# Seven block products in place of eight for half of a down-projection, put between the pieces of the next up-projection

## The chip, the cores and the metric

The kernel runs on one core of a Trainium2 chip. The metric is the device time of one launch in microseconds (us). Matmuls run on TensorE (PE; its weight loads are shown as PEld), elementwise work on VectorE (DVE) and ScalarE (ACT), and all transfers are issued from SyncE's queue (SP).

## The reference

One layer of a hybrid encoder, for a sequence of 256 tokens and a width of 2,048, all in float32. An attention block comes first (eight heads of forgetting attention, eight of stick-breaking attention), then the block that the change is about, a feed-forward block with a short convolution:

```python
def conv_ffn(h, w_up_l, conv_w_l, conv_b_l, w_down_l):
    u = h @ w_up_l                       # (256, 2048) @ (2048, 2 * 5632)
    u = lax.conv_general_dilated(...) + conv_b_l   # causal, depthwise, width 3
    gate, val = jnp.split(u, 2, axis=-1)
    return (jax.nn.silu(gate) * val) @ w_down_l    # (256, 5632) @ (5632, 2048)

x = x + hybrid_mixer(rms_norm(x, attn_norm), ...)
x = x + conv_ffn(rms_norm(x, ffn_norm), w_up, conv_w, conv_b, w_down)
```

## The kernel before

A float32 matmul is made of three matmuls of a rounded type: each operand is split into a high part (`hi`, the value rounded) and a low part (`lo`, what is left), and the products hi x hi, hi x lo and lo x hi are summed in PSUM.

`weights` (L202) brings in every weight: 1 MB (128 partitions of 2,048 values) goes by DMA into one of three `w_raw` buffers, ScalarE casts it into one of two `w_hi` buffers (L210), and VectorE subtracts to make one of two `w_lo` buffers (L211). Its three instructions are written at a raised priority (`AHEAD`), so that the scheduler puts them ahead of other work. The scheduler of the framework sets the order on each engine when the kernel is built, from priorities, from data and from buffers coming free; on the chip each engine runs its list in order.

Two shapes of matmul use these weights. `feature_major` (L242) makes the up-projection: two feature tiles of 128 for all 256 tokens, in two steps of 32 matmuls (16 with a moving operand of 512 columns, L250, 16 of 256, L255), each with one load of weights. `token_major` (L220) makes 512 output columns for two token tiles: each load of weights serves four row tiles, so a chunk is 4 x 2 x 3 = 24 matmuls of 512 columns (L235 to L237). After each step or chunk both call `step()`, which advances generators that hold other work, here the last of the attention.

The feed-forward block takes its 44 feature tiles in three parts of 16, 16 and 12. In each part, pairs of feature tiles come first: `up_pair` for the gate and for the value, `convolved` (L582: the sum of two PSUM halves, the norm's factor `R`, the three taps), SiLU, product, and the split into `g2`, whose tiles wait for the down-projection. Then the part's down-projection runs, four groups of 512 columns, each added to the residual rows `x2` (L630). After the last part each group is stored. The up accumulators rotate over three buffers of two PSUM banks.

The memory is handed out in pools. `const`, `wpool` (the weight buffers), `big` (`x2`, the transposed input `hT`) and `small` live through the kernel; `at` and `tmp` belong to the attention and are closed at its end. The pool `ff` of the feed-forward block is opened after that, on their ground; its first instructions are the MEMSETs of `up` (L579). The attention ends with the out-projection (`token_major` with `oT`, of which the last four tiles lie in `hT`), the update of the rows (L556), the squares of the new rows (L167, into `junk` in `tmp`), and the transposes into `hT` (L152). `crow`, the convolution's parameters, is loaded early (L118, L119) and transposed after the first pair.

Of the kernel before, what the change touches and what calls it, by code (L numbers as in the profile page):

```python
# [11 lines left out]
ALU = mybir.AluOpType  # L12
# [27 lines left out]
FFN_PARTS = [(0, 16), (16, 32), (32, 44)]  # L40
# [3 lines left out]
def hybrid_layer(  # L44
# [28 lines left out]
    wpool = ctx.enter_context(tc.tile_pool(name="wpool", bufs=3))  # L73
# [5 lines left out]
    def f32(t):  # L79
        return t.bitcast(F32)  # L80
# [5 lines left out]
    crow = const.tile([NC2, 4, P], F32, name="crow")  # L86
# [94 lines left out]
    def in_every_partition(dg, n):  # L181
        R = const.tile([P, S], F32, name=f"R{n}")
# [19 lines left out]
    def weights(src, a, b):  # L202
        raw = wpool.tile([P, 2048], F32, name="w_raw", tag="w_raw")
        hi = wpool.tile([P, 2048], F32R, name="w_hi", tag="w_hi", bufs=2)
        lo = wpool.tile([P, 2048], F32R, name="w_lo", tag="w_lo", bufs=2)
        n = a * b
        r3 = raw[:, :n].rearrange("p (a b) -> p a b", a=a)
        with tc.high_priority(offset=AHEAD):
            nc.sync.dma_start(r3, src)
            act.copy(hi[:, :n], raw[:, :n])  # L210
            dve.tensor_tensor(lo[:, :n], raw[:, :n], f32(hi[:, :n]), op=ALU.subtract)  # L211
# [57 lines left out]
    with ExitStack() as actx:  # L269
        at = actx.enter_context(tc.tile_pool(name="at", bufs=1))  # L270
# [201 lines left out]
        R1 = in_every_partition(dg1, 1)  # L472
        R1q = const.tile([P, S], F32, name="R1q")
# [92 lines left out]

    def convolution_parameters():
# [6 lines left out]
    ff = ctx.enter_context(tc.tile_pool(name="ff", bufs=2))  # L574
    psf = ctx.enter_context(tc.tile_pool(name="psf", bufs=1, space=bass.MemoryType.PSUM))
    nu = 4
    up = [ff.tile([P, 2, 2 + S], F32, name=f"up{i}") for i in range(nu)]
    for u in up:
        dve.memset(u[:, :, 0:2], 0.0)  # L579
    n_up = 0  # L580

    def convolved(ps, f0):  # L582

        nonlocal n_up
        u = up[n_up % nu]
# [3 lines left out]
        a = ff.tile([P, 2, S], F32, name="cv", tag="cv", bufs=4)  # L589
# [13 lines left out]
    def up_pair(f0):  # L603

        nonlocal R, n_pair
        pool, tag = (psf, "pu") if n_pair % 3 == 2 else (psa, "acc")
        n_pair += 1
        acc = feature_major(wu, f0 * P, pool, tag)
        if R is None:
            R = in_every_partition(dg2, 2)  # L610
            convolution_parameters()
        return convolved(acc, f0)

    gT = {}
    n_pair = 0
    for n_part, (f_lo, f_hi) in enumerate(FFN_PARTS):
        for f in range(f_lo, f_hi, 2):
            gate = up_pair(f)
            val = up_pair(NFT + f)
            act.activation(gate, gate, AF.Silu)  # L620
            dve.tensor_tensor(gate, gate, val, op=ALU.mult)
            g2 = ff.tile([P, 2, 2, S], F32R, name="g2", tag="g2", bufs=12)
            act.copy(g2[:, 0], gate)  # L623
            dve.tensor_tensor(g2[:, 1], gate, f32(g2[:, 0]), op=ALU.subtract)
            for j in range(2):
                gT[f + j] = g2[:, :, j, :]
        for c in range(4):
            acc = token_major(lambda k: gT[f_lo + k], wd, f_lo, f_hi - f_lo, 512 * c, 512)
            xs = x2[:, :, c * 512 : (c + 1) * 512]
            dve.tensor_tensor(xs, acc, xs, op=ALU.add)  # L630
            if n_part == len(FFN_PARTS) - 1:
                for t in range(NT):
                    nc.sync.dma_start(of[t * P : (t + 1) * P, c * 512 : (c + 1) * 512], xs[:, t, :])
# [57 lines left out]
```

## Time and profile before

| | |
|---|---|
| median of 3 runs | 1152.66 us (1152.63 to 1153.39) |
| the profiled execution | 1153.37 us |
| its span, first to last instruction | 1151.6 us |
| the out-projection ends, the first up step begins | 412.9 us from the start of the span |
| the first part's down-projection begins | 593.3 us |
| moved by DMA | 211.39 MB, mean 184 GB/s |

In the rows of the profile a line stands as "L250", then the engine, the operation, output<-inputs, the count and the busy time. A timeline row begins with the start and the duration in us. A row of busy times by stretch has, after the stretch and its length, the busy time of PE, PEld, DVE, ACT and POOL, each with the count of its instructions, then the granted TensorE clock, the DMA share and GB/s. A wait has the waiting instruction, what it waited for, the total in us, how often, and the longest.

### The profile page before, as it was taken

To read this page: it belongs to the slowest core of one execution; us is meant where nothing else is said; L and a number is where in the kernel's file an instruction comes from. 1 tells how busy PE (TensorE), PEld (TensorE's weight loads), DVE (VectorE), ACT (ScalarE), POOL (GpSimd) and SP (SyncE) were. 2 spreads that over 40 slices of the span, in tenths; PEclk is the share of its full clock that TensorE was granted. 3 is DMA by queue.
4 is the path that set the end of the run, shared out by engine and by line. 5 is a ranking of instruction groups with operands and counts; after the bars stand their busy time and mean duration, and the time that the engine had idled before them with its cause. 6 is when DMAs were issued, how large, how long until landed. Compare 5 with 4: busy or idle time off the path is not lost.

```text
span 1151.6 us, 14371 instructions
## 1 busy us (share of the span) xinstructions
PE 1137.1 (99%) x6002; PEld 976.7 (85%) x6002; DVE 716.4 (62%) x798; ACT 551.9 (48%) x620; POOL 0.2 (0%) x4
## 2 busy tenths in 40 slices
PE   7999999999999999999999999999999999999998
PEld 5998888888888888888888888888888888888886
DVE  4646756646565667677774546767775455767753
ACT  4644454455564555555554334555554334555531
POOL 0000000000000000000000000000000000000000
PEclk9999999999999999999999999999999999999999
DMA  6766555564445545555556655555556655555562
GB/s 227 213 210 204 170 173 161 168 182 148 147 149 170 185 154 193 195 194 185 183 183 198 203 183 186 194 196 192 184 183 188 204 193 183 187 195 193 189 221 74
DMA packets 162540, 211.39 MB, mean 184 GB/s; under 512 B 3737, under 2 KB 117547, under 8 KB 162475
## 3 DMA queue, kind: packets, MB, share of 16 engines
q1 hardware_dynamic: 162474, 210.47, 56.7%
q8 instruction: 47, 0.77, 0.3%
q14 instruction: 19, 0.15, 0.0%
HBM read 208.36 MB, written 2.10 MB: 183 GB/s over the span
## 4 chain that ended last, share of the span: by engine, by line
PE 96%; DVE 1%; ACT 1%; DMA 1%; issue 1%; SPq 0%; ACTq 0%; DVEq 0%
PE pu L250 34%; PE pu L255 17%; PE acc L236 14%; PE acc L237 14%; PE acc L235 14%; ACT w_hi L210 1%; DVE w_lo L211 1%; PE ps_x L152 1%; DMA w_raw<-in_w_in_dram 0%; DMA masks<-in_cst_dram 0%; PE ps_z L492 0%; PE ps_h L284 0%; PE ps_s L425 0%; PE ps_o L452 0%; PE ps_o L518 0%
## 5 line engine op out<-in xcount | busy, mean ns | idle before, releaser
L211 DVE TENSOR_TENSOR w_lo<-w_raw,w_hi 128x2048 fp32r<-128x2048 f32 (+2 forms) x204 | 450.8, 2210 | 360.2 <-ACT w_hi L210 360.2
L210 ACT CAST w_hi<-w_raw 128x2048 fp32r<-128x2048 f32 (+2 forms) x204 | 375.9, 1843 | 512.4 <-issue 260.5
L250 PE MATMUL pu<-hT,w_hi 128*128 128x512 f32 x1664 | 523.5, 396 | 0.0
L255 PEld LDWEIGHTS pu<-hT,w_lo 128*128 128x128 f32 x1664 | 312.4, 188 | 73.9 <-DVE w_lo L211 0.4
L255 PE MATMUL pu<-hT,w_lo 128*128 128x256 f32 x1664 | 327.6, 278 | 0.0
L250 PEld LDWEIGHTS pu<-hT,w_hi 128*128 128x128 f32 x1664 | 253.8, 189 | 0.3
L236 PE MATMUL acc<-w_lo,g 128*128 128x512 f32 x352 | 137.1, 389 | 0.8 <-DVE w_lo L211 0.8
L235 PE MATMUL acc<-w_hi,g 128*128 128x512 f32 x352 | 137.1, 389 | 0.0
L237 PE MATMUL acc<-w_hi,g 128*128 128x512 f32 x352 | 136.9, 389 | 0.0
L235 PE MATMUL acc<-w_hi,hT 128*128 128x512 f32 (+1 forms) x320 | 120.2, 376 | 0.0
L236 PE MATMUL acc<-w_lo,hT 128*128 128x512 f32 (+1 forms) x320 | 119.2, 373 | 0.5 <-DVE w_lo L211 0.3
L237 PE MATMUL acc<-w_hi,hT 128*128 128x512 f32 (+1 forms) x320 | 119.0, 372 | 0.0
L236 PEld LDWEIGHTS acc<-w_lo,g 128*128 128x128 f32 x352 | 66.1, 188 | 14.8 <-DVE w_lo L211 1.3
L235 PEld LDWEIGHTS acc<-w_hi,g 128*128 128x128 f32 x352 | 66.1, 188 | 13.8 <-ACT g L623 0.3
L237 PEld LDWEIGHTS acc<-w_hi,g 128*128 128x128 f32 x352 | 66.1, 188 | 13.8
L597 DVE SCALAR_TENSOR_TENSOR cv<-up,ccol,cv 128x256 f32<-128x256 f32 x176 | 74.2, 480 | 2.2 <-ACT cv L592 2.0
L236 PEld LDWEIGHTS acc<-w_lo,hT 128*128 128x128 f32 x320 | 60.5, 189 | 9.6 <-DVE w_lo L211 1.5
L237 PEld LDWEIGHTS acc<-w_hi,hT 128*128 128x128 f32 x320 | 60.6, 189 | 8.8
L235 PEld LDWEIGHTS acc<-w_hi,hT 128*128 128x128 f32 x320 | 60.6, 189 | 8.1
L592 ACT ACTIVATE cv<-up,ccol 128x256 f32<-128x256 f32 x88 | 48.2, 591 | 8.0 <-DVE up L588 8.0
L235 PE MATMUL acc<-w_hi,oT 128*128 128x512 f32 x96 | 38.1, 397 | 0.0
L237 PE MATMUL acc<-w_hi,oT 128*128 128x512 f32 x96 | 37.5, 390 | 0.0
(146 smaller groups left out, 602.4 us busy)
## 6 DMA issues: line engine op xcount, KB each, us to landing
w_raw<-in_w_up_dram SPq DMA_DIRECT2D x88, 1024.0 KB, 5.1
w_raw<-in_w_down_dram SPq DMA_DIRECT2D x44, 1024.0 KB, 5.1
w_raw<-in_w_in_dram SPq DMA_DIRECT2D x36, 1024.0 KB, 5.3
w_raw<-in_w_out_dram SPq DMA_DIRECT2D x16, 1024.0 KB, 5.1
w_raw<-in_w_in_dram SPq DMA_DIRECT2D x12, 688.0 KB, 4.3
w_raw<-in_w_in_dram SPq DMA_DIRECT2D x8, 512.0 KB, 5.3
out_dram<-x SPq DMA_DIRECT2D x8, 256.0 KB, 3.6
x<-in_x_dram SPq DMA_DIRECT2D x3, 512.0 KB, 6.2
```

The lines of the kernel that those rows point to most:

```text
L152: nc.tensor.transpose(ps[:, j, t * P : (t + 1) * P], xt[t][:, (k + j) * P : (k + j + 1) * P], ident)
L210: act.copy(hi[:, :n], raw[:, :n])
L211: dve.tensor_tensor(lo[:, :n], raw[:, :n], f32(hi[:, :n]), op=ALU.subtract)
L235: nc.tensor.matmul(o, lhi, hi[:, i, :], start=first, stop=False)
L236: nc.tensor.matmul(o, lhi, lo[:, i, :], start=False, stop=False)
L237: nc.tensor.matmul(o, llo, hi[:, i, :], start=False, stop=last)
L250: nc.tensor.matmul(acc[:, j, :], hi[:, i, j * P : (j + 1) * P], hT[:, k].rearrange("p a b -> p (a b)"), start=k == 0, stop=False,)
L255: nc.tensor.matmul(acc[:, j, S:], lo[:, i, j * P : (j + 1) * P], hT[:, k, 0, :], start=False, stop=k == KT - 1,)
L592: act.activation(a[:, j, :], u[:, j, 2:], AF.Identity, scale=ccol[:, 2, f : f + 1], bias=ccol[:, 3, f : f + 1],)
L597: dve.scalar_tensor_tensor(a[:, j, :], u[:, j, w : w + S], ccol[:, w, f : f + 1], a[:, j, :], op0=ALU.mult, op1=ALU.add,)
```

## The change

The parts are now five of eight feature tiles and one of four. The down-projection of a part is no longer run at the part's end: it is put into a queue of two generators, `behind`, and `step()` takes the next piece of it at a set pace while the next part's up-projection runs. What is left at the end of that part is run there; the last part's down-projection runs at the end, as before.

For columns 0 to 1,023 the piece is one of seven block products (`down_in_seven`). The 256 x 1,024 by 1,024 x 1,024 product is seen as 2 x 2 blocks (tokens, features, columns), and Winograd's form of Strassen's scheme makes it from seven block products rather than eight: on sums of the activations' blocks (`combinations`, made once a part) and on sums of the weights' blocks (`w_sum`). Each product is 12 matmuls into one of three PSUM banks, which is added to or subtracted from the rows after each product. For columns 1,024 to 2,047 the pieces are chunks of 24 matmuls as before (`down_plain`).

The buffers change with it. The pool of weight buffers is closed with the attention, and the feed-forward block opens one of its own, `wff`, with four `w_raw`, three `w_hi`, three `w_lo` and one `w_sum`. `crow` moves into `ff` and is loaded at the start of the feed-forward block; `R1` and `R1q` move into `at`. The up accumulators rotate over two buffers rather than three, the `up` tiles are two rather than four, gate and value get tags of their own (three and one). `step()` of this block advances all waiting generators, not two.

```diff
-FFN_PARTS = [(0, 16), (16, 32), (32, 44)]
+FFN_PARTS = [(f, min(f + 8, NFT)) for f in range(0, NFT, 8)]
...
-    wpool = ctx.enter_context(tc.tile_pool(name="wpool", bufs=3))
...
-        nc.sync.dma_start(crow[:, :3, :], conv_w[0].rearrange("w (n p) -> n w p", p=P))
-        nc.sync.dma_start(crow[:, 3, :], conv_b[0].rearrange("(n p) -> n p", p=P))
...
+    def load(src, into=None):
+        raw = into if into is not None else wpool.tile([P, 2048], F32, name="w_raw", tag="w_raw")
+        a, b = src.shape[1:]
+        nc.sync.dma_start(raw[:, : a * b].rearrange("p (a b) -> p a b", a=a), src)
+        return raw
+
+    def split(raw, a, b):
+        hi = wpool.tile([P, 2048], F32R, name="w_hi", tag="w_hi", bufs=n_split)
+        lo = wpool.tile([P, 2048], F32R, name="w_lo", tag="w_lo", bufs=n_split)
...
+    def weights(src, a, b):
+        with tc.high_priority(offset=AHEAD):
+            return split(load(src), a, b)
...
     with ExitStack() as actx:
+        n_split = 2
+        wpool = actx.enter_context(tc.tile_pool(name="wpool", bufs=3))
         at = actx.enter_context(tc.tile_pool(name="at", bufs=1))
...
+    n_split = 3
+    wpool = ctx.enter_context(tc.tile_pool(name="wff", bufs=4))
+    ff = ctx.enter_context(tc.tile_pool(name="ff", bufs=2))
+    psf = ctx.enter_context(tc.tile_pool(name="psf", bufs=2, space=bass.MemoryType.PSUM))
+    crow = ff.tile([NC2, 4, P], F32, name="crow", tag="val", bufs=1)
+    nc.sync.dma_start(crow[:, :3, :], conv_w[0].rearrange("w (n p) -> n w p", p=P))
+    nc.sync.dma_start(crow[:, 3, :], conv_b[0].rearrange("(n p) -> n p", p=P))
+    up = [ff.tile([P, 2, 2 + S], F32, name=f"up{i}", bufs=1) for i in range(2)]
...
+    def step():
+        nonlocal n_behind
+        for g in list(waiting):
+            if next(g, g) is g:
+                waiting.remove(g)
+        n_behind += pace
+        while behind and n_behind >= 16:
+            n_behind -= 16
+            if next(behind[0], behind) is behind:
+                behind.popleft()
...
+    def combinations(g1, g2):
+        a11, a21 = g1[:, :, :P], g1[:, :, P:]
+        a12, a22 = g2[:, :, :P], g2[:, :, P:]
+        s = ff.tile([P, 2, 4, 2, P], F32R, name="s", tag="s")
+        t = [ff.tile([P, 2, 2, P], F32, name="t2", tag="t2") for _ in range(2)]
+        t5, s2, s4, t7 = t[0][:, 0], t[0][:, 1], t[1][:, 0], t[1][:, 1]
+        dve.tensor_tensor(t5, a21, a22, op=ALU.subtract)
+        dve.tensor_tensor(s2, t5, a11, op=ALU.subtract)
+        dve.tensor_tensor(s4, a12, s2, op=ALU.add)
+        dve.tensor_tensor(t7, a11, a21, op=ALU.subtract)
+        for i in range(2):
+            act.copy(s[:, 0, 2 * i : 2 * i + 2], t[i])
+            dve.tensor_tensor(
+                s[:, 1, 2 * i : 2 * i + 2], t[i], f32(s[:, 0, 2 * i : 2 * i + 2]), op=ALU.subtract
+            )
+        return s
+
+    def down_in_seven(f0, pairs, sums, c0):
...
+        def product(bank, first, lhs, parts):
+            hi, lo = parts
+            for i in range(4):
+                a, j = divmod(i, 2)
+                for n, (l, r) in enumerate(((0, hi), (0, lo), (1, hi))):
+                    nc.tensor.matmul(
+                        bank, lhs(a, l, j), r[:, i, :], start=first and i + n == 0,
+                        stop=i == 3 and n == 2, skip_group_check=not first,
+                    )
...
+        bank_a = psf.tile([P, 512], F32, name="bank_a", tag="a")
+        with ahead():
+            w = wpool.tile([P, 2048], F32, name="w_sum", tag="w_sum", bufs=1)
+            load(w11, into=w)
+            parts = split(w, 4, 512)
+        product(bank_a, True, of_pairs(0, 0), parts)
+        add(x11, bank_a)
+        yield
+        bank_b = psb.tile([P, 512], F32, name="bank_b", tag="t")
+        with ahead():
+            dve.tensor_tensor(w, w, load(w12), op=ALU.add)
+            parts = split(w, 4, 512)
+        product(bank_b, True, of_sums(0), parts)
+        add(x22, bank_b)
+        yield
...
+    def down_plain(f0, pairs, c0, cols):
+        for c in range(c0, c0 + cols, 512):
+            acc = [psf.tile([P, 512], F32, name="bank_a", tag="a") for _ in range(NT)]
+            for k0 in range(0, 2 * len(pairs), 4):
+                hi, lo = weights(rows_of(wd, f0 + k0, 4, c, 512), 4, 512)
...
     for n_part, (f_lo, f_hi) in enumerate(FFN_PARTS):
+        pairs, gates, sums = [], [], []
+        last_part = n_part == len(FFN_PARTS) - 1
+        pace = (11 if behind and len(behind) == 2 else 16) * 8 // (f_hi - f_lo)
         for f in range(f_lo, f_hi, 2):
...
+            if len(pairs) > 2:
+                sums.append(combinations(gates[-3], gate))
+        while behind:
+            n_behind, pace = 16, 0
+            step()
+        if not last_part:
+            behind.append(down_in_seven(f_lo, pairs, sums, 0))
+            behind.append(down_plain(f_lo, pairs, 1024, 1024))
```

More of the change, by code (lines that the diff above doesn't have):

```diff
@@ L85, in hybrid_layer @@
     prow = const.tile([50, P], F32, name="prow")
-    crow = const.tile([NC2, 4, P], F32, name="crow")
     bf = const.tile([P, NH], F32, name="bf")
@@ L199, in finish @@
             step()
[L202 to L205, printed above, removed]
-        n = a * b
[L207 to L211, printed above, removed]
+    def load(src, into=None):
[6 more added lines that the diff above has]
+        lo = wpool.tile([P, 2048], F32R, name="w_lo", tag="w_lo", bufs=n_split)
+        n = a * b
+        act.copy(hi[:, :n], raw[:, :n])
+        dve.tensor_tensor(lo[:, :n], raw[:, :n], f32(hi[:, :n]), op=ALU.subtract)
         return (
@@ L571, in convolution_parameters, with convolved @@
             dve.tensor_copy(ccol[:, i, :], pc[:, :NC2])
[L574 to L582, printed above, removed]
+    def convolved(ps, f0, tag, bufs):
         nonlocal n_up
-        u = up[n_up % nu]
+        u = up[n_up % 2]
         n_up += 1
@@ L601, in convolved @@
         return a
[L603 to L608, printed above, removed]
+    behind = deque()
+    n_behind, pace = 0, 0
+    def step():
[8 more added lines that the diff above has]
+                behind.popleft()
@@ new lines, in down_plain @@
+    def down_plain(f0, pairs, c0, cols):
[3 more added lines that the diff above has]
+                hi, lo = weights(rows_of(wd, f0 + k0, 4, c, 512), 4, 512)
+                for i in range(4):
+                    k = k0 + i
+                    first, last = k == 0, k == 2 * len(pairs) - 1
+                    g = pairs[k // 2][:, :, k % 2, :]
+                    for t in range(NT):
+                        ts = slice(t * P, (t + 1) * P)
+                        nc.tensor.matmul(acc[t], g[:, 0, ts], hi[:, i, :], start=first, stop=False)
+                        nc.tensor.matmul(acc[t], g[:, 0, ts], lo[:, i, :], start=False, stop=False)
+                        nc.tensor.matmul(acc[t], g[:, 1, ts], hi[:, i, :], start=False, stop=last)
+                if last:
+                    for t in range(NT):
+                        xs = xt[t][:, c : c + 512]
+                        dve.tensor_tensor(xs, acc[t], xs, op=ALU.add)
+                yield
@@ L623, in hybrid_layer @@
             act.copy(g2[:, 0], gate)
             dve.tensor_tensor(g2[:, 1], gate, f32(g2[:, 0]), op=ALU.subtract)
[L625 to L633, printed above, removed]
+            pairs.append(g2)
@@ new lines, in hybrid_layer @@
+            gates.append(gate)
+            if len(pairs) > 2:
[6 more added lines that the diff above has]
+            behind.append(down_plain(f_lo, pairs, 1024, 1024))
+    for c in range(4):
+        acc = token_major(
+            lambda k: pairs[k // 2][:, :, k % 2, :], wd, f_lo, f_hi - f_lo, 512 * c, 512
+        )
+        xs = x2[:, :, c * 512 : (c + 1) * 512]
+        dve.tensor_tensor(xs, acc, xs, op=ALU.add)
+        for t in range(NT):
+            nc.sync.dma_start(of[t * P : (t + 1) * P, c * 512 : (c + 1) * 512], xs[:, t, :])
```

72 lines of the change are left out of this document (60 added, 12 removed).

## The prediction

> **What bounds the kernel now.** I read the page first: the engines' busy time, the chain that ended last, the costly groups and the DMA issues.
>
> ```profile
> span 1151.6 us, 14371 instructions
> ...
> PE 1137.1 (99%) x6002; PEld 976.7 (85%) x6002; DVE 716.4 (62%) x798; ACT 551.9 (48%) x620; POOL 0.2 (0%) x4
> ...
> PE 96%; DVE 1%; ACT 1%; DMA 1%; issue 1%; SPq 0%; ACTq 0%; DVEq 0%
> ...
> L210 ACT CAST w_hi<-w_raw 128x2048 fp32r<-128x2048 f32 (+2 forms) x204 | 375.9, 1843 | 512.4 <-issue 260.5
> ...
> w_raw<-in_w_up_dram SPq DMA_DIRECT2D x88, 1024.0 KB, 5.1
> ```
>
> TensorE is busy for 99% of the span and carries 96% of the chain. Next I asked for the waits of TensorE from 420 us on, which is the whole ConvFFN, and for the engines' busy time in a stretch of up-projection alone and in one of down-projection alone.
>
> ```profile
> PE acc L236 <- DVE w_lo L211: 0.8, 1, 0.8
> ```
>
> ```profile
> 460.00:590.00 130.00, 130.00 (x748) 113.48 (x747) 93.81 (x104) 68.77 (x71) 0.00 (x0) 1.00 0.58 191
> 600.00:670.00 70.00, 70.00 (x311) 57.97 (x310) 36.16 (x22) 25.60 (x16) 0.00 (x0) 1.00 0.59 192
> ```
>
> In 730 us the matrix engine waits 0.8 us in all, so a matmul taken away here is time won as long as the others keep up. VectorE (the third busy column) is the next engine: 93.81 of 130 us in the up-projection, but 36.16 of 70 us in the down-projection.
>
> **The matmuls removed.** In the down-projection two splits in a row on VectorE stand one chunk of 24 matmuls apart (four row tiles, two token tiles, three products each); in the up-projection two casts in a row on ScalarE stand one step of 32 apart.
>
> ```profile
> 1121.00 2.29 DVE L211 TENSOR_TENSOR w_lo<-w_raw,w_hi 128x2048 fp32r<-128x2048 f32 x1 [3.15 <-ACT w_hi L210]
> 1126.44 2.29 DVE L211 TENSOR_TENSOR w_lo<-w_raw,w_hi 128x2048 fp32r<-128x2048 f32 x1 [3.15 <-ACT w_hi L210]
> ```
>
> ```profile
> 576.58 1.91 ACT L210 CAST w_hi<-w_raw 128x2048 fp32r<-128x2048 f32 x1 [2.65 <-issue]
> 582.16 1.91 ACT L210 CAST w_hi<-w_raw 128x2048 fp32r<-128x2048 f32 x1 [2.67 <-issue]
> ```
>
> A chunk is 1126.44 - 1121.00 = 5.44 us, so a matmul of 512 columns costs 0.227 us of the engine (the 389 ns that a single one lasts overlap). A step of the up-projection is 5.58 us. A block product is 12 matmuls, 2.72 us. Half of the columns of a part of eight feature tiles were eight such products and are now seven; five parts have them, the last part of four tiles has not. So 5 x 12 = 60 matmuls go: 60 x 0.227 = **-13.6 us**. The other 1,024 columns, the last part, and the up-projection have the matmuls they had.
>
> **VectorE's new work.** The prices are in the groups of 460 to 590 us.
>
> ```profile
> L211 DVE TENSOR_TENSOR w_lo<-w_raw,w_hi 128x2048 fp32r<-128x2048 f32 x24 | 55.0, 2293 | 35.8 <-ACT w_hi L210 35.8
> L597 DVE SCALAR_TENSOR_TENSOR cv<-up,ccol,cv 128x256 f32<-128x256 f32 x44 | 18.3, 479 | 0.0
> ...
> L266 DVE TENSOR_TENSOR t<-pu,t 128x512 f32<-128x512 f32 x12 | 8.2, 685 | 0.0
> ...
> L624 DVE TENSOR_TENSOR g<-cv,g 128x512 fp32r<-128x512 f32 x6 | 4.1, 684 | 0.0
> ```
>
> An up step costs VectorE 93.81 x 5.58 / 130 = 4.03 us. For the seven products it now makes seven splits in place of four and four weight sums of the same shape (no sum of this kind is in the trace; the split is its nearest row): 11 x 2.29 = 25.2 us. Each product is added to the rows, 128x512 from PSUM like L266: 7 x 0.69 = 4.8 us. A pair of `combinations` is four small differences and two subtractions, 4 x 0.48 + 2 x 0.68 = 3.3 us.
>
> At a pace of 11 in 16 the seven products fall behind up steps 2, 3, 5, 6, 8, 9 and 11. Up to step 12, with the first `combinations`, VectorE has 12 x 4.03 + 25.2 + 4.8 + 3.3 = 81.7 us of work, and TensorE 12 x 5.58 + 7 x 2.72 = 86.0 us: 95% full. Over the part, with four plain chunks (four splits, four adds, the second `combinations`), it is 113 of 130 us, 87%. In the last part the pace is 22, and the seven products fall within six steps: 6 x 4.03 + 30.0 = 54.2 us against 6 x 5.58 + 19.0 = 52.5 us.
>
> Does that hold TensorE up? A third pair of `w_hi`, `w_lo` lets the split of an item begin when the item three before it is done. Two items lie between, an up step and a product at the least in the parts of eight: 8.3 us, for a cast of 1.91 and a subtraction of 2.29 us. The splits go ahead of other work, so what is pushed back is the rest: the reading of the up accumulators (now two, so each has a whole pair of steps, 11.2 us, to be read in), the adds (a bank is written again a step or more later), and the activations that the next part wants only after its second step. I take 0 here. The bounds are 0 and, in the last part, the 1.7 us that the work exceeds the cover; if the waits in VectorE's own queue do not shrink the price is larger, and that is a rival below. ScalarE gets three casts more, 5.7 us a part, and is at 68.77 of 130 us. The loads are six a part for the seven products in place of four, 10 MB more over the kernel at a DMA share of 0.58: hidden.
>
> In the last part alone two plain chunks on the same two banks follow each other with no step between. The second must wait for two adds of the first; by the rows of L556 below (0.26 us until the add starts, 0.70 us each) the first bank is free some 0.5 us late, and up to 2.3 us later if a split is ahead. I take **+0.5 us**.
>
> **The border between attention and ConvFFN.** This is the term that no word of the change announces. Before, one pool held the weight buffers through the whole kernel. Now it closes with the attention, and the ConvFFN's buffers come from a new pool that is laid over the old weight pool and part of `at`. What such a border does can be read off the pool `ff` of the kernel before, laid over the same kind of ground. Its first instructions are the MEMSETs of `up`, which need no data.
>
> ```profile
> 4.00 0.23 DVE L355 CAST identR<-cs 128x128 fp32r<-128x128 f32 x1 [4.00 <-DMA cs<-in_cst_dram]
> ...
> 396.95 2.29 DVE L211 TENSOR_TENSOR w_lo<-w_raw,w_hi 128x2048 fp32r<-128x2048 f32 x1 [3.19 <-ACT w_hi L210]
> ...
> 413.12 1.41 DVE L556 SCALAR_TENSOR_TENSOR x<-acc,rg,x 128x512 f32<-128x512 f32 x2 [0.26 <-PE acc L237]
> ...
> 417.42 0.07 DVE L579 MEMSET up<- 128x4 f32 x2
> ```
>
> ```profile
> 416.12 0.19 ACT L167 ACTIVATION_READ_ACCUMULATOR junk<-x 128x1 f32 x1
> ```
>
> The schedule does pull work forward into a gap: the cast of `identR`, written after a whole projection, is the first thing VectorE does. The MEMSETs were not put into the 3.19 us gap at 394, nor any other, but came after the last use of the old pools at 416.3 us. So I read it that a new pool waits for the old ones it covers as a whole. Then no weight of the up-projection can be loaded before the last matmul of the out-projection.
>
> ```profile
> 412.69 0.39 PE L237 MATMUL acc<-w_hi,hT 128*128 128x512 f32 x1
> 412.92 0.62 PE L250 MATMUL pu<-hT,w_hi 128*128 128x512 f32 x2
> 413.37 0.40 PE L255 MATMUL pu<-hT,w_lo 128*128 128x256 f32 x2
> ...
> 418.49 1.04 PE L152 MATMUL ps_x<-cs,x 128*128 128x128 f32 x8
> 419.28 0.70 PE L250 MATMUL pu<-hT,w_hi 128*128 128x512 f32 x2
> ```
>
> Before, the up-projection follows at once, its weights having been loaded, cast and split. After: last matmul done at 412.69 + 0.39 = 413.1, load 5.1, cast 1.91, subtraction 2.29, so the first L255 at 422.4 in place of 413.4: 9.0 us. On SyncE's queue the next loads stand behind that first one; on ScalarE and VectorE their splits; on TensorE everything. The transposes of the last columns (419.28 - 418.49 = 0.8 us) can move into the gap: **+8.2 us**. Bounds: 0 if slots are handed over one by one, 11.4 if the pool also waits for the squares at 416.3.
>
> A gap that long has a second price. At the start the first matmuls are slow, after waits of microseconds:
>
> ```profile
> PE pp L142 <- DMA prow<-in_attn_norm_dram: 4.3, 1, 4.3
> PE ps_x L152 <- DMA x<-in_x_dram: 3.1, 1, 3.1
> ```
>
> ```profile
> 10.22 0.80 PE L236 MATMUL acc<-w_lo,hT 128*128 128x512 f32 x1
> ...
> 11.23 0.63 PE L235 MATMUL acc<-w_hi,hT 128*128 128x512 f32 x1
> ...
> 13.37 0.63 PE L237 MATMUL acc<-w_hi,hT 128*128 128x512 f32 x1
> ...
> 14.49 0.48 PE L235 MATMUL acc<-w_hi,hT 128*128 128x512 f32 x1
> ```
>
> ```profile
> 10.00:14.00 4.00, 3.94 (x10) 2.94 (x10) 2.57 (x5) 1.55 (x3) 0.00 (x0) 1.00 0.83 272
> ```
>
> Five intervals between 11.23 and 13.37 make 0.43 us each, against 0.227 later, although the granted clock of that stretch is given as 1.00; from 10.22 to 14.49 that loses 4.27 x (1 - 0.227/0.43) = 2.0 us. After the start no wait of TensorE reaches 1 us, so the trace does not show whether the rate falls again; the bounds are 0 and 2.0. I take **+2.0 us**, since the gap at the border is longer than the waits that come before those slow matmuls. The Trainium skill's page "TensorE: Matmul & The Clock Gate" (Part 1, the HAM clock gate) speaks against the change here: after an idle window of about 3.4 us the array goes back to half its clock, and takes about as long a busy one to leave it; by its figure the price would be an estimated 1.6 us, and the sum 0.4 us lower. The slow start agrees with it, the granted clock of 1.00 does not.
>
> The loads of `crow` move from the start to this border, behind the first weights on SyncE's queue; they are wanted after the first pair of up steps (about 435 us), and even three loads of 5.1 us ahead of them let them land before. The end is as it was: last add, store.
>
> Sum: -13.6 + 0.5 + 8.2 + 2.0 = -2.9 us. The profiled execution took 1153.37 us (span 1151.6), so 1150.5; it lies 0.7 us over the median of the runs shown, 1152.66, against which the forecast is **1149.8 us**.
>
> **Rivals.** *The border is free* (chance 0.18): the pool's slots are handed over singly, the loads run ahead as before, and neither the 8.2 nor the 2.0 us is paid: 1152.66 - 13.6 + 0.5 = 1139.6 us. For it: before, three buffers always run ahead. Against it: the MEMSETs.
>
> *VectorE's queue becomes the bound* (0.27), the one that ends slower. Its work runs in the order issued, and each subtraction waits for its cast. Now that wait is 35.8 / 24 = 1.49 us a split, which idle time pays for. In steps 1 to 12 there are 19 splits and 86.0 - 81.7 = 4.3 us of room, so it decides from 0.23 us a split on. If a quarter of today's wait stays, 0.37 us, a part of eight loses 19 x 0.37 - 4.3 = 2.7 us, four of them 10.9, and the last part 13 x 0.37 + 1.7 = 6.5: 1149.8 + 17.4 = 1167.2 us. For it: 95% and 103% full. Against it: splits have 8.3 us where they need 4.2, and a busier queue arrives later at each subtraction, when the cast is done.
>
> **How the numbers follow.** The forecast has 0.55, its own range 1147 to 1155 (both bounds of the clock term, a border up to 11.4, the last part's 1.7). About 0.2% (2.3 us) is what a measurement of this kernel can tell from no change: below 1150.4, above 1155.0. The forecast lies at that edge: of its 0.55, 0.25 are faster, 0.25 the same, 0.05 slower. With the rivals: faster 0.43, same 0.25, slower 0.32. The range runs from the free border, 1139.6, to 1163, within the second rival (at 0.32 us a split), which leaves about 0.2 outside.
>
> **What would show it.** Right: 5,942 instructions on TensorE (6,002 - 60); after the out-projection's last matmul a gap of about 9 us on TensorE, ended by a load of `w_raw`, then some ten matmuls at 0.43 us; VectorE 80 to 90% busy in parts two to five, with TensorE waiting under a microsecond a part. Wrong: up weights issued before the out-projection ends (first rival); TensorE's waits in the ConvFFN ended by `w_lo`, several us a part, worst in the last (second rival); or products spaced wider than 0.227 us a matmul, which would undo the first term.

## The result

The changed kernel took 1242.01 us (median of 4 runs, 1241.55 to 1242.52), the kernel before 1152.94 us (4 runs, 1152.63 to 1153.39): a ratio of 1.0772, 95% interval 1.0754 to 1.0791. The forecast was 1149.8 us with a range up to 1163.0, so the change is slower by 89 us where a small gain was expected. The profiled execution took 1241.73 us.

The page of the kernel after, in its lines of the span, the busy times, TensorE's share in 40 slices of 31 us with the granted clock below it, and the chain that ended last:

```profile
span 1239.8 us, 14496 instructions
...
PE 1152.9 (93%) x5942; PEld 973.4 (79%) x5942; DVE 843.2 (68%) x938; ACT 591.4 (48%) x655; POOL 0.2 (0%) x4
...
PE   7999999999999899879996999968999699996997
...
PEclk9999999999999899989998999989999899998999
...
PE 78%; DVE 14%; ACT 4%; issue 3%; DMA 1%; SPq 0%; ACTq 0%; DVEq 0%
```

TensorE has the 5,942 instructions that were predicted, 60 fewer, yet it is busy for longer, idle for 7% of the span, and carries 78% of the chain in place of 96%. The loss is not spread out: from slice 16 on, five dips to 6 or 7 tenths of full use recur, with stretches at 9 between them. The waits of TensorE count the same five:

```profile
PE bank_a L673 <- DVE x L679: 46.8, 5, 9.4
PE bank_c L673 <- ACT w_hi L208: 7.8, 5, 1.6
PE pu L252 <- ACT w_hi L208: 6.4, 4, 2.0
PE pu L252 <- DVE t L268: 5.5, 5, 1.1
```

L673 is the matmul of a block product, L679 the `add` of a bank to the rows. Once a part, TensorE stands for 9.4 us before a product that wants a bank back which has not yet been added. TensorE's timeline of part two shows the place (columns: start, duration, then the instruction):

```profile
514.79 0.39 PE L673 MATMUL bank_a<-w_hi,g 128*128 128x512 f32 x1
516.28 0.70 PE L252 MATMUL pu<-hT,w_hi 128*128 128x512 f32 x2 [1.10 <-DVE t L268]
...
523.09 0.39 PE L673 MATMUL bank_b<-w_hi,s 128*128 128x512 f32 x1
532.85 0.77 PE L673 MATMUL bank_a<-w_hi,s 128*128 128x512 f32 x1 [9.37 <-DVE x L679]
533.42 0.63 PE L673 MATMUL bank_a<-w_lo,s 128*128 128x512 f32 x1
```

The first product ends at 515, an up step follows, and the first half of the second product, the six matmuls that read the first `s`, ends at 523. The next matmuls in TensorE's list belong to product four, which wants `bank_a` back, and stand until 532.85. From there on to 577 the other products and all four plain chunks follow each other with a single matmul of an up step among them (at 566.10); then the remaining up steps of the part run alone. In busy times by stretch (PE, PEld, DVE, ACT, POOL, then the granted clock, the DMA share and GB/s):

```profile
512.00:532.00 20.00, 10.38 (x53) 8.22 (x51) 20.00 (x19) 8.72 (x9) 0.00 (x0) 0.89 0.47 158
532.00:538.00 6.00, 5.15 (x12) 3.60 (x13) 4.73 (x10) 1.76 (x3) 0.00 (x0) 0.51 0.00 0
578.00:640.00 62.00, 62.00 (x359) 54.09 (x357) 42.72 (x46) 31.59 (x31) 0.00 (x0) 1.00 0.59 191
```

In the first, VectorE is busy for 20.00 of 20 us and TensorE for 10.38. In the second, behind the gap, TensorE works at a granted clock of 0.51. In the third, up-projection alone, VectorE has 42.72 of 62 us: the room that the products needed, after they were done. What VectorE did before the late `add`:

```profile
517.85 2.28 DVE L209 TENSOR_TENSOR w_lo<-w_sum,w_hi 128x2048 fp32r<-128x2048 f32 x1
520.06 2.28 DVE L209 TENSOR_TENSOR w_lo<-w_raw,w_hi 128x2048 fp32r<-128x2048 f32 x1
522.26 2.28 DVE L703 TENSOR_TENSOR w_sum<-w_sum,w_raw 128x2048 f32<-128x2048 f32 x1
...
526.84 2.28 DVE L209 TENSOR_TENSOR w_lo<-w_sum,w_hi 128x2048 fp32r<-128x2048 f32 x1
529.04 0.47 DVE L605 SCALAR_TENSOR_TENSOR val<-up,ccol,val 128x256 f32<-128x256 f32 x1
529.43 2.28 DVE L723 TENSOR_TENSOR w_sum<-w_sum,w_raw 128x2048 f32<-128x2048 f32 x1
531.64 0.47 DVE L605 SCALAR_TENSOR_TENSOR val<-up,ccol,val 128x256 f32<-128x256 f32 x1
532.03 0.68 DVE L679 TENSOR_TENSOR x<-x,bank_a 128x512 f32<-128x512 f32 x1
...
535.73 1.29 DVE L649 TENSOR_TENSOR s<-t,s 128x512 fp32r<-128x512 f32 x2 [0.22 <-ACT s L648]
```

The bank was full at 515 and is added at 532.03, behind splits and weight sums of 2.28 us each for products two, three, four and seven, which stand at the raised priority. Behind it in the same queue comes the second `s` of the part, made from its last pair of feature tiles (L649, 535.73); the second halves of products two to five read it, so they could not have run before then either.

Why are the products in a crowd? The cause stands in the diff. `step()` does `n_behind += pace` whether or not anything waits in `behind`. Part one has 16 up steps, a pace of 16 and an empty queue: it leaves a credit of 256. At the first step of part two the loop `while behind and n_behind >= 16` hands out all 13 pieces (seven products and four chunks, and the two calls that find a generator ended) and keeps 256 + 11 - 13 x 16 = 59; the rest of that part brings it to 224. Followed through by hand, the pieces of the later parts come out like this:

```
pieces handed out after each up step
part two    13 0 0 0 0 0 0 0 0 0 0 0 0 0 0 0    credit left 224
part three  13 0 0 0 0 0 0 0 0 0 0 0 0 0 0 0                192
part four   12 1 0 0 0 0 0 0 0 0 0 0 0 0 0 0                160
part five   10 1 1 0 1 0 0 0 0 0 0 0 0 0 0 0                128
last part    9 1 2 1 0 0 0 0                                 96
```

So the change does not do what its words say. The experiments test this against the rival that the crowd does no harm and only an order of VectorE's queue does, and price what is left once the crowd is gone.

### The profile page after: what moved, and what is told of

Read it like the earlier page. It is cut to its first block, busy times and chain, and to the rows that moved or that the text cites. A ratio compares the mean times of both kernels' runs of the same rounds, so it can differ in the third digit from the quotient of the medians.

```text
span 1239.8 us, 14496 instructions
## 1 busy us (share of the span) xinstructions
PE 1152.9 (93%) x5942; PEld 973.4 (79%) x5942; DVE 843.2 (68%) x938; ACT 591.4 (48%) x655; POOL 0.2 (0%) x4
## 4 chain that ended last, share of the span: by engine, by line
PE 78%; DVE 14%; ACT 4%; issue 3%; DMA 1%; SPq 0%; ACTq 0%; DVEq 0%
PE pu L252 24%; PE pu L257 12%; PE acc L238 7%; PE acc L237 7%; PE acc L239 7%; DVE w_lo L209 6%; PE bank_a L673 4%; ACT w_hi L208 4%; PE bank_a L745 3%; PE bank_a L746 3%; PE bank_a L744 3%; PE bank_b L673 2%; DVE val L605 1%; PE bank_c L673 1%; DVE w_raw L714 1%
## 5 line engine op out<-in xcount | busy, mean ns | idle before, releaser
L209 DVE TENSOR_TENSOR w_lo<-w_raw,w_hi 128x2048 fp32r<-128x2048 f32 (+2 forms) x199 | 439.1, 2206 | 310.3 <-ACT w_hi L208 310.2
L673 PE MATMUL bank_a<-w_hi,s 128*128 128x512 f32 x80 | 32.8, 463 | 46.8 <-DVE x L679 46.8
L745 PE MATMUL bank_a<-w_lo,g 128*128 128x512 f32 x160 | 64.0, 400 | 0.0
L744 PE MATMUL bank_a<-w_hi,g 128*128 128x512 f32 x160 | 63.9, 399 | 0.0
L746 PE MATMUL bank_a<-w_hi,g 128*128 128x512 f32 x160 | 63.2, 399 | 0.0
L673 PEld LDWEIGHTS bank_a<-w_hi,s 128*128 128x128 f32 x80 | 18.0, 225 | 52.9 <-issue 48.8
L208 ACT CAST w_hi<-w_sum 128x2048 fp32r<-128x2048 f32 x20 | 38.1, 1905 | 29.6 <-DVE w_sum L703 16.8
L209 DVE TENSOR_TENSOR w_lo<-w_sum,w_hi 128x2048 fp32r<-128x2048 f32 x20 | 45.7, 2286 | 5.6 <-ACT w_hi L208 5.6
L605 DVE SCALAR_TENSOR_TENSOR gate<-up,ccol,gate 128x256 f32<-128x256 f32 x88 | 37.5, 479 | 1.6 <-ACT gate L600 1.3
L605 DVE SCALAR_TENSOR_TENSOR val<-up,ccol,val 128x256 f32<-128x256 f32 x88 | 37.7, 479 | 0.7 <-ACT val L600 0.7
L237 PE MATMUL acc<-w_hi,oT 128*128 128x512 f32 x96 | 38.1, 397 | 0.0
```

Source lines behind the costliest of these rows:

```text
L237: nc.tensor.matmul(o, lhi, hi[:, i, :], start=first, stop=False)
L605: dve.scalar_tensor_tensor(a[:, j, :], u[:, j, w : w + S], ccol[:, w, f : f + 1], a[:, j, :], op0=ALU.mult, op1=ALU.add,)
L673: nc.tensor.matmul(bank, lhs(a, l, j), r[:, i, :], start=first and i + n == 0, stop=i == 3 and n == 2, skip_group_check=not first,)
L744: nc.tensor.matmul(acc[t], g[:, 0, ts], hi[:, i, :], start=first, stop=False)
L745: nc.tensor.matmul(acc[t], g[:, 0, ts], lo[:, i, :], start=False, stop=False)
L746: nc.tensor.matmul(acc[t], g[:, 1, ts], hi[:, i, :], start=False, stop=last)
```

## The experiments

### The pace alone

```diff
-        n_behind += pace
+        n_behind = n_behind + pace if behind else 0
```

> The changed kernel with one line different: step() counts up only while something is in the queue, so that the pieces come one by one as the pace of 11 in 16 says. Theory A (the credit saved up in a part with an empty queue lets all thirteen pieces out at the first step of the next part, and the crowd is what costs): TensorE's wait of 9.4 us a part for the add to the rows goes, and so do most of the 101.8 us (1239.8 - 1151.6 + 13.6) that the span is over what the fewer matmuls should give; what stays is the border's 8 to 11 us: 1147 to 1158 us. Theory B (VectorE's work for seven products is too much wherever it is put): the same work at 95% of the cover still holds TensorE up, 1167 us or more.

Measured: 1163.85 us (1162.67 to 1165.48) against 1152.3, a ratio of 1.0099 (1.0084 to 1.0114). One line gives back 78.2 of 89 us. The busy times of most of a part from product one on (120 of 131 us), and the two longest waits of its up steps:

```profile
663.30:783.40 120.10, 120.10 (x630) 101.86 (x629) 99.24 (x99) 64.58 (x59) 0.00 (x0) 1.00 0.64 212
```

```profile
PE pu L252 <- DVE t L268: 5.7, 1, 5.7
...
PE pu L257 <- DVE w_lo L209: 1.1, 1, 1.1
```

TensorE is busy for all of 120.10 us, with VectorE at 99.24, 83%. The four lines of waits above, 66.5 us together, are gone but for one of 5.7 us and one of 0.5. Another 17.5 us are in TensorE's busy time, which falls from 1152.9 to 1135.4 us for the same instructions: the slow matmuls behind the waits (mean granted clock over the span: 0.972 with the crowd, 0.992 without). The credit is the cause. But 1163.85 lies 6 us over what theory A allowed, under the 1167 of theory B, and 11.6 us over the kernel before: something is left.

### The order on VectorE's queue

The adds at the raised priority, with the crowd as it was:

```diff
         def add(to, bank, op=ALU.add):
-            dve.tensor_tensor(to, to, bank, op=op)
+            with ahead():
+                dve.tensor_tensor(to, to, bank, op=op)
```

> The changed kernel, pieces still let out all at once, but the adds of a product's bank to the rows written at the raised priority. Order theory (the adds stand too late in VectorE's queue, behind splits and sums, and that alone holds TensorE): the five waits of 9.4 us go, 46.8 us, and the slow matmuls behind them: 1180 to 1195 us. Work theory (seven splits, four sums and seven adds, 30 us of VectorE, for 19 us of matmuls with hardly an up step between): the wait moves to the next w_lo or w_hi, and the time falls by less than 15 us: above 1227 us.

Measured: 1241.98 us (1240.33 to 1242.86), a ratio of 1.0774 (1.0758 to 1.079): no gain. The add of the first product comes at 515.44 in place of 532.03, and the wait moves on:

```profile
PE bank_b L673 <- ACT s L648: 22.6, 5, 4.5
PE bank_a L673 <- ACT w_hi L208: 12.4, 5, 2.5
PE bank_a L673 <- DVE w_lo L209: 9.0, 5, 1.9
```

The largest wait is now for the second `s` of the part. The line with the largest wait of the kernel after names the instruction that came last, not the amount of work: seven splits, four sums and seven adds beside 19 us of products, and the last pair of the part before in the same queue.

### The border alone

The kernel before, with its weight pool closed after the attention and a new one opened, and nothing else:

```diff
-    wpool = ctx.enter_context(tc.tile_pool(name="wpool", bufs=3))
...
     with ExitStack() as actx:
+        wpool = actx.enter_context(tc.tile_pool(name="wpool", bufs=3))
...
+    wpool = ctx.enter_context(tc.tile_pool(name="wff", bufs=3))
     ff = ctx.enter_context(tc.tile_pool(name="ff", bufs=2))
```

> The kernel before, its weight pool closed with the attention and a new one of the same size opened for the ConvFFN; nothing else. If a new pool waits for the old ones as a whole: the first load of up weights comes after the last matmul of the out-projection, 8.2 us of gap and up to 2.0 us of slow matmuls, 1161 to 1164 us. If slots are handed over singly: 1153 us.

Measured: 1162.23 us (1161.92 to 1162.4), a ratio of 1.0084 (1.0067 to 1.0101): 9.9 us more, where the prediction had 8.2 + 2.0 = 10.2. TensorE's timeline at the border, the loads on SyncE's queue and the busy times of two stretches:

```profile
411.79 0.39 PE L236 MATMUL acc<-w_hi,hT 128*128 128x512 f32 x1
413.02 0.44 PE L151 MATMUL ps_x<-cs,x 128*128 128x128 f32 x2 [0.85 <-DVE x L556]
...
420.46 1.19 PE L249 MATMUL pu<-hT,w_hi 128*128 128x512 f32 x2
422.39 0.80 PE L254 MATMUL pu<-hT,w_lo 128*128 128x256 f32 x2 [0.74 <-DVE w_lo L210]
422.99 1.05 PE L249 MATMUL pu<-hT,w_hi 128*128 128x512 f32 x2
```

```profile
412.21 12.88 SPq L208 DMA_DIRECT2D w_raw<-in_w_up_dram  x5
```

```profile
413.00:422.00 9.00, 4.81 (x18) 2.89 (x18) 6.43 (x22) 6.62 (x12) 0.00 (x0) 0.63 1.04 331
422.00:426.00 4.00, 3.61 (x12) 3.17 (x13) 2.70 (x3) 0.30 (x1) 0.00 (x0) 0.55 0.74 247
```

The first load of an up weight is issued at 412.21, as the out-projection's last matmul (411.79 + 0.39) ends, not a microsecond earlier, though the last split of the old `w_raw` had ended at 404.7. The first L254 comes at 422.39; 422.4 was worked out. That the two agree to the hundredth is luck: the out-projection ended 0.9 us earlier than in the kernel before, and the split began 0.8 us late, behind VectorE's copies of the convolution's parameters. And the clock falls: 0.63 and 0.55 are granted in the 13 us behind the out-projection.

The gap is not the empty stretch of 9 us that the prediction expected. Other work moves into it (transposes, the norm's factor, the parameters), and the longest wait is 3.02 us. In the profiled executions, which lie 8.5 us apart, TensorE is idle 5.1 us longer than before (19.6 against 14.5 us), and busy 3.4 us longer (1140.5 against 1137.1) for the same instructions.

### The border taken away

The paced kernel, but the old pool (three `w_raw`, two `w_hi`, two `w_lo`) stays open, and the new pool adds a fourth, a third and a third, taken in turn:

```diff
+    wpool = ctx.enter_context(tc.tile_pool(name="wpool", bufs=3))
...
+            raw = (wff if n_raw % 4 == 0 and wff is not None else wpool).tile(...)
...
+        third = n_cut % 3 == 0 and wff is not None
+        pool, bufs = (wff, 1) if third else (wpool, 2)
...
+    wff = ctx.enter_context(tc.tile_pool(name="wff", bufs=1))
```

> The paced kernel with the old weight pool kept open to the end; the new pool adds only the fourth w_raw, the third w_hi and w_lo, and w_sum, and the buffers are taken in turn from both. If the border is the 9.9 us that the kernel before loses by it (1162.2 against 1152.3): the up weights are loaded ahead again and the paced kernel's 1163.9 falls to 1153 to 1155 us. If the border costs less here, because the pace or VectorE would have held TensorE anyway: above 1158 us.

Measured: 1154.96 us (1154.03 to 1156.86) against 1152.63, a ratio of 1.0023 (1.0014 to 1.0032): 8.9 us less than with the border. The forecast's 13.6 us of matmuls are still not to be seen.

### No products, only the interleaving

The paced kernel with all 2,048 columns of the down-projection as plain chunks:

```diff
-            if len(pairs) > 2:
-                sums.append(combinations(gates[-3], gate))
...
-            behind.append(down_in_seven(f_lo, pairs, sums, 0))
-            behind.append(down_plain(f_lo, pairs, 1024, 1024))
+            behind.append(down_plain(f_lo, pairs, 0, 2048))
```

> The paced kernel with all columns as plain chunks, none as seven products (no sums of weights or activations): 60 matmuls more than the changed kernel. Theory A: only the border is left of the costs, 1152.9 + 8 to 11 = 1161 to 1164 us, and the paced kernel with seven products is up to 13.6 us under it. If putting pieces between up steps itself costs (two up accumulators, one val buffer): above 1168 us.

Measured: 1172.8 us (1171.67 to 1173.47), a ratio of 1.0174 (1.0159 to 1.019). With the matmuls of the kernel before and its border priced, 1162.2 was due; 10.6 us are missing although VectorE has less to do. Where a kernel without products loses, products are not the cause. The time lies in the range of the rival, that the interleaving itself costs, but most of the loss turned out to be something else: its 1,056 matmuls of the down-projection come at 0.2333 us in place of 0.2267, worth 7.0 us (the next section has the reason; this kernel was not run at the other rate), and its profile has two waits before the last down-projection, 1.9 and 1.6 us, for 3.5.

### The rate of the down-projection's matmuls

The starts of 16 matmuls in a row of the kernel before span 640.01 to 643.41 for 15 intervals, 0.2267 us each. Those of the paced kernel, 750.08 to 754.98 for 21, are 0.2333 us (first and last shown). In the prediction's words, products "wider than 0.227 us a matmul".

```profile
640.01 0.39 PE L237 MATMUL acc<-w_hi,g 128*128 128x512 f32 x1
...
643.41 0.39 PE L237 MATMUL acc<-w_hi,g 128*128 128x512 f32 x1
```

```profile
750.08 0.39 PE L745 MATMUL bank_a<-w_lo,g 128*128 128x512 f32 x1
...
754.98 0.39 PE L745 MATMUL bank_a<-w_lo,g 128*128 128x512 f32 x1
```

The durations are the same 0.39 us, and the rate of the up-projection is the same too (5.57 us a step). What differs is the place of the stationary operand, the one that is loaded as weights, here `g2` or `s`: by the sizes of the tiles laid out ahead of it, it begins at a remainder of 352 bytes modulo 512 in the kernel before and of 160 in the kernel after. The `up` tiles lie ahead of it, so columns added to them that nothing reads shift it without touching any instruction's place in its queue. The first guess was that the remainder modulo 128 decides (96 before, 32 after). Three kernels tested that:

```diff
# shifted, in the paced kernel and in the one without border
-    up = [ff.tile([P, 2, 2 + S], F32, name=f"up{i}", bufs=1) for i in range(2)]
+    up = [ff.tile([P, 2, 8 + S], F32, name=f"up{i}", bufs=1) for i in range(2)]
# kernel before, shifted by two buffers
-    up = [ff.tile([P, 2, 2 + S], F32, name=f"up{i}") for i in range(nu)]
+    up = [ff.tile([P, 2, 2 + S], F32, name=f"up{i}", bufs=2 if i < 2 else 1) for i in range(nu)]
```

> The paced kernel with its two up tiles six columns wider, so that g2 and s begin 64 bytes higher in each partition, at the remainder modulo 128 that g2 had in the kernel before; every engine's list is the same. In the paced kernel a matmul of 512 columns on g2 or s takes 0.2333 us of TensorE, in the kernel before 0.2267. Place theory (where the stationary operand lies makes this difference): 996 x 0.0066 = 6.6 us less, 1156 to 1158 us. If the difference comes from the other engines' load or the order of the matmuls: 1163 to 1165 us.

> Both edits on the paced kernel: two pools and the 64 bytes. If border and place are separate costs and add up: 1163.9 - 9.9 - 6.6 = 1147 us (1145.5 to 1149), 0.4% under the kernel before. What would be left of the 13.6 us is then eaten by one stop of TensorE of 5.7 us for the reading of an up accumulator. If VectorE's work is what holds the kernel: above 1155 us.

> The kernel before with two of the four up tiles given one buffer in place of two, which moves g2 by 4,160 bytes, to the remainder 32 modulo 128 that it has in the changed kernel; every engine's list is the same. Place theory: the 1,056 matmuls on g2 go from 0.2267 to 0.2333 us, 1152.3 + 7.0 = 1159 us. If the place does nothing: 1152 to 1153 us.

Measured: 1163.57 us (ratio 1.0094, 1.0081 to 1.0107), 1155.41 us (1.0026, 1.0016 to 1.0036) and 1154.47 us (1.0019, 1.001 to 1.0028). The guess falls: at 96 modulo 128 the interval stayed at 0.2326 us in the first two, and the kernel before lost 1.8 us where it should have lost 7.0. (The first two times lie in the ranges of their rivals, the order of the matmuls and VectorE's work; with the rate hardly changed they decide nothing about those.) But the kernel before did lose, with its instructions in the same order, and its interval was 0.2290 us at a remainder of 288. So the two remainders that were known were given to the other kernel: 352 to the one without border, 160 to the kernel before.

```diff
# the kernel without border, at 352
+    up = [ff.tile([P, 2, 16 + S], F32, name=f"up{i}", bufs=1) for i in range(2)]
# the kernel before, at 160
+    up = [ff.tile([P, 2, 10 + S], F32, name=f"up{i}", bufs=2 if i < 2 else 1) for i in range(nu)]
```

> The paced kernel with two pools (1155.0 us), its up tiles widened so that g2 and s begin at the remainder 352 modulo 512 that g2 has in the kernel before; every engine's list is the same. So far a matmul on g2 took TensorE 0.2267 us at remainder 352, 0.2290 at 288, 0.2326 at 224 and 0.2334 at 160. If the place of the stationary operand sets this: 0.2267 again, 996 x 0.0067 = 6.7 us less, 1147.5 to 1149.5 us. If it is something else that differs between the two kernels: 0.233 us, and 1154 to 1156 us.

> The kernel before with g2 at the remainder 160 modulo 512 (two up tiles with one buffer, all four wider); every engine's list is the same as before. If the place sets the rate: 0.2334 us a matmul, 1152.6 + 1056 x 0.0067 = 1159.7 us. If not: 0.2267 to 0.229 us, 1152.5 to 1154.5 us.

Measured: 1147.81 us (1146.95 to 1153.31; ratio 0.9966, 0.9953 to 0.9978), 7.2 us less than before the shift; and 1159.39 us (1158.52 to 1159.86; ratio 1.0059, 1.0047 to 1.0071), 6.8 us more than the kernel before. Both hit. The kernel before at 160, beside its rows above, has 15 intervals of 0.2333 us:

```profile
640.29 0.39 PE L237 MATMUL acc<-w_hi,g 128*128 128x512 f32 x1
...
643.79 0.40 PE L237 MATMUL acc<-w_hi,g 128*128 128x512 f32 x1
```

The changed kernel has 5 x (84 + 96) + 96 = 996 such matmuls; at 0.0066 us each that is 6.6 us. Other tiles moved along with `g2`, but from 612 to 666 us of the kernel before at 160 VectorE and ScalarE work only on weights and on the rows, which did not move: of what moved, TensorE's stationary operand alone is in use there.

### The one stop that was left

The 5.7 us are at 541 us of the paced kernel, in part two. VectorE and ScalarE there:

```profile
538.92 0.69 DVE L649 TENSOR_TENSOR s<-t,s 128x512 fp32r<-128x512 f32 x1
...
542.91 0.68 DVE L649 TENSOR_TENSOR s<-t,s 128x512 fp32r<-128x512 f32 x1
...
543.51 2.29 DVE L209 TENSOR_TENSOR w_lo<-w_raw,w_hi 128x2048 fp32r<-128x2048 f32 x1
545.71 0.68 DVE L268 TENSOR_TENSOR t<-pu,t 128x512 f32<-128x512 f32 x1
```

```profile
541.09 1.89 ACT L208 CAST w_hi<-w_raw 128x2048 fp32r<-128x2048 f32 x1
542.89 0.57 ACT L267 COPY t<-pu 128x512 f32<-128x512 f32 x1
```

L267 and L268 read an up accumulator out of PSUM, into a tile of tag `t2`. `combinations` takes its two intermediate tiles from the same tag, which has two buffers. The buffers go round in the order of the program, in which `combinations` comes before the next accumulator. That accumulator was full at 523.5, but the combinations stood late in VectorE's queue, and the first of their tiles is given back with the first L649, at 539.6. By then ScalarE has two casts before its L267, at 542.89, and VectorE a split before its L268, at 545.71; until that is done TensorE has no accumulator to write to. A tag of its own removes this (the memory for it comes from the fourth `w_raw`, which is given up):

```diff
-        t = [ff.tile([P, 2, 2, P], F32, name="t2", tag="t2") for _ in range(2)]
+        t = [ff.tile([P, 2, 2, P], F32, name="t3", tag="t3") for _ in range(2)]
```

> The paced kernel with two pools, where the combinations get buffers of their own in place of the two t2 that the up accumulators are also read into (and the fourth w_raw is left out, for the room). If the one stop of 5.7 us is an accumulator that cannot be read because the combinations hold both t2: the stop goes, 1149 to 1150 us. If VectorE's queue is late anyway: the same stop, 1154 to 1156 us.

> Both together. If place and shared buffers are separate costs: 1155.0 - 6.7 - 5.7 = 1142.6 us (1141 to 1145), 0.9% under the kernel before, 3 us over what 60 fewer matmuls could give at most. If neither: 1154 to 1156 us.

Measured: the kernel without border, with the tag of its own, 1145.83 us (1144.97 to 1146.73), a ratio of 0.9941 (0.9928 to 0.9954); with the remainder of 352 too, 1139.55 us (1139.17 to 1140.31), a ratio of 0.9888 (0.9875 to 0.9901). Both are below what was expected: the tag's 9.1 us are more than the stop of 5.7 us. The kernel that still has the stop shows the main reason, TensorE empty for a stretch and then at half its clock:

```profile
533.00:538.00 5.00, 0.00 (x0) 0.00 (x0) 5.00 (x4) 3.10 (x4) 0.00 (x0) 0.75 0.36 99
538.00:542.00 4.00, 3.41 (x10) 2.95 (x11) 3.93 (x8) 1.66 (x4) 0.00 (x0) 0.50 1.05 384
```

Another 0.6 us is a wait for `crow` at the border, which went as well. In all, TensorE's idle time falls by 6.4 us between the two profiles and its busy time by 2.7 (1132.4 to 1129.7). The edit has two parts, and the fourth `w_raw` was not put back to see its share.

The last of these kernels beats both that the case began with. Its page, and the busy times of 440 us of its ConvFFN:

```profile
PE 1122.7 (99%) x5942; PEld 964.7 (85%) x5942; DVE 838.1 (74%) x938; ACT 591.9 (52%) x655; POOL 0.2 (0%) x4
```

```profile
600.00:1040.00 440.00, 440.00 (x2328) 377.05 (x2327) 371.65 (x376) 236.26 (x213) 0.00 (x0) 1.00 0.62 206
```

TensorE is busy for 440.00 of 440 us, beside a VectorE at 84%. It lies 13.0 us below the kernel before, for 60 matmuls fewer; TensorE's busy time is 14.4 us less (1122.7 against 1137.1).

## Why the prediction was wrong, step by step

**The matmuls removed, -13.6 us: right.** 13.0 us are what the best version gains, though the same version with plain chunks was not run. The kernel after could not show them, since TensorE was no longer the only bound.

**"At a pace of 11 in 16 the seven products fall behind up steps 2, 3, 5, 6, 8, 9 and 11": the step that failed.** It took the pace from `pace = ...` and began its count at zero with part two. The counter comes in with 256, and the products fall behind step 1. No profile was needed: the line `n_behind += pace` stands in the diff outside the loop that tests `behind`. The step costs 1242.0 - 1163.85 = 78.2 us. The rival that belonged here, that the change doesn't do what it says, was not among the rivals.

**VectorE keeps up, 0 us: right, for the spread that it assumed.** Over 120 us of a part it is 83% full, by a working that said 87% for the part, and the paced kernel waits for no split in the parts after the second. In part two the same 0 was wrong once: it rested on each up accumulator having 11.2 us to be read in, which left out that the reading needs a free `t2` (below). The second rival, VectorE's queue as the bound at a spread pace, falls with that. In the kernel after VectorE is the bound, but in stretches of some tens of microseconds and because of the crowd.

**The border, +8.2 and +2.0 us: right in sum, not in its parts.** 9.9 us together, by the border alone, and 8.9 less in the paced kernel without it. The reading of the MEMSETs, that a new pool waits for the pools beneath it as a whole, is borne out, and the free border falls. But it is 5.1 us of idle time and 3.4 of longer busy time: the gap was priced too high and the slow clock, at its upper bound of 2.0, too low. Between 422.99 and 424.27 matmuls of 512 columns make 0.43 us each, in a stretch with a granted clock of 0.55. The Trainium skill's "TensorE: Matmul & The Clock Gate" (Part 1, the HAM clock gate) has half the clock after an idle window of about 3.4 us. Most of these runs agree: the clock fell in gaps of 9.4 and 5.7 us, and behind one of 1.99 us, in the kernel after, the matmuls went on at 0.23 us:

```profile
566.10 0.50 PE L252 MATMUL pu<-hT,w_hi 128*128 128x512 f32 x1 [1.99 <-ACT w_hi L208]
566.44 0.40 PE L744 MATMUL bank_a<-w_hi,g 128*128 128x512 f32 x1
566.68 0.39 PE L745 MATMUL bank_a<-w_lo,g 128*128 128x512 f32 x1
```

The border alone fits only if its eight transposes do not count as work, which no run here tests: its longest wait is 3.02 us, and the granted clock is down at 0.50 from 416 to 417 us, before that wait is over, but nearly 4 us after the out-projection's last matmul. The estimate of 1.6 us by that page and the 2.0 taken both lie under the 3.4 us of longer busy time.

**The bank used again, +0.5 us: right** (0.6 us in the last part of the paced kernel, before the second plain chunk). The profile names ScalarE's `val` as what came last there, but that touches neither the bank nor an operand of the matmul; the add that frees the bank (L750) ends at 1121.93, and the matmul starts at 1122.07.

**Two terms were not in the sum.** The shared tag `t2` in `combinations` costs about 8 us: the stop of 5.7 and the slow clock after it. The line stands in the diff. The place of `g2` and `s` costs 6.6 us, and nothing in the trace of before could show it. With them, both sized after the fact, the paced kernel adds up: 1152.3 - 13.6 + 9.9 + 8 + 6.6 = 1163.2 us, against 1163.85 measured. Even with the pace as it was read, then, the forecast of 1149.8 us would have been 14 us short.

## What to carry to other kernels

Follow a counter that paces interleaved work by hand through every stage, from its first value on and through the stages in which its queue is empty, before pricing the interleaving. Look for what a new user of a buffer's tag keeps from the old ones, and count a pool opened over closed ones, in a pipeline that loads ahead, as an emptied pipeline with a slow clock behind it. Where a wait names one instruction on a full engine, changing the order there moves the wait; only spreading the work removes it.

## What the hardware showed that was not expected

A matmul of 512 columns, issued with a weight load each, followed the one before at an interval that depends on where its stationary operand begins in a partition: 0.2267 us at a remainder of 352 bytes modulo 512, 0.2290 at 288, 0.2326 at 224, 0.2333 at 160. The kernel before has the same instructions in the same order at 352, 288 and 160. Moved from 352 to 160 it takes 6.8 us longer, three times what a measurement of this kernel can tell from no change. The moving operand, the weights, stayed where it was. Why the place matters was not settled; four remainders were seen and no rule is drawn from them.
